# A conformer trunk step: the first two channel tiles projected from unscaled input

## The chip, the cores and the metric

The kernel runs as one program on one core of a Trainium2 chip. The metric is the device time of one execution in microseconds (us). The engines of the core work side by side, each through its own instructions in order: PE (TensorE, matmuls and weight loads), DVE (VectorE), ACT (ScalarE), POOL (GpSimd) and SP (SyncE), which here issues most DMAs.

## The reference, cut to what matters

Eight running streams of 16 new frames and one prompt of 512 frames go through a conformer layer, an attention layer and two feed-forward blocks. What the change touches is the head of the conformer layer:

```
def rms_norm(x, g):
    y = xf * lax.rsqrt(jnp.mean(xf * xf, axis=-1, keepdims=True) + EPS)
    return (y * g.astype(jnp.float32)).astype(x.dtype)

def conv_module(h, hist, g, w_pw1, b_pw1, w_dw, b_dw, ln_g, ln_b, w_pw2, b_pw2):
    a, gate = jnp.split(rms_norm(h, g) @ w_pw1 + b_pw1, 2, axis=-1)
    glu = a * jax.nn.sigmoid(gate)
    full = jnp.concatenate([hist.astype(glu.dtype), glu], axis=1)
    y = lax.conv_general_dilated(full, w_dw[:, None, :], ..., feature_group_count=D_MODEL) + b_dw
    y = jax.nn.silu(layer_norm(y, ln_g, ln_b))
    return h + y @ w_pw2 + b_pw2, full[:, -CONV_HIST:]
```

The model width is 1024. The factor of the norm, one number for each frame, is the same for all channels, so it may be multiplied in before or behind the projection; the gain `g`, one number for each input channel, must be in before it.

## The kernel before

**Layout.** Channels lie on the 128 partitions, in eight channel tiles (`KT`); frames lie along the free dimension. There are NT = 640 frames (128 of the streams, 512 of the prompt), cut into two groups of 320 (`GS`). `h` holds x. Every matmul that must be exact is made of three: an operand is split into a rounded high part and a low remainder (`xh`, `xl` of the input by `xsplit`, `whi`, `wlo` of the weights by `wsplit`), and `mm3` (lines 196 to 202) adds high by high, low weight by high input and high weight by low input. So one product of a tile of 128 output channels and a group takes 24 matmuls of 320 columns, and a channel tile of the gated projection, which has a value half and a gate half, takes 48 for each group.

**Order.** `PLAN` (line 72) is an order written out by hand, one letter for each step of `step` (line 987): `a0` is tile 0 for group 0, `y` loads the second half of x, `x1` is tile 1 for group 0 with the second group's norm inside it, `b0` and `b1` are tiles 0 and 1 for group 1, `q0` the depthwise convolution of tile 0 on POOL (`conv_pool`, whose inputs ACT makes), `dp1s0` a convolution on DVE, `c2` tile 2 for both groups, and so on. The tiling framework then places the instructions on the engines in the order of its own estimate; `high_priority` moves an instruction forward in it, and `behind` or `issue_after` ties an instruction behind another of the same engine, with no wait between engines.

**The first norm.** `rms` (line 292) calls `rstd_bc` (line 268): `square` for each tile of x on ACT or DVE (`SSQ`), a running sum `acc` on DVE for group 0 (`colmean`, line 219), three one-column matmuls that turn the sum into means, an added epsilon (`rst`, line 275), the power -1/2 on POOL (line 282), and `spread` (line 250), which copies the factor to all partitions in PSUM. Then, tile by tile, `n` (line 303) multiplies x, gain and factor on DVE, ACT rounds it to `xh` (line 187), and DVE makes `xl` (line 189). For group 1 the running sum is made on POOL. The first projection `glu_` (line 752) takes `xs[0]`, the result for group 0; the value half and the gate half are two `mm` tiles, of which there are four.

**Fillings.** `warm(n)` (line 143) issues n matmuls of the identity, each shown as two in the profile; `WARM = 30, 9, 5, 5` places them at the start, behind group 0's means, and behind each of the two spreads.

**Weights.** `wsplit` loads 1 MB for each tile into `raw` and splits it; for tiles 0 and 1 in four quarters (`cuts=4`, lines 732 and 737), whose order is tied to the norm's steps. `PL1 = (0, 2, ...)` puts half of tile 1's low parts on POOL. There are two buffers each of `raw`, `whi` and `wlo`.

**Tap weights.** `conv_load` (line 839) makes on POOL the tap weights of tiles whose convolution runs on PE, into three `w4` buffers. Those three buffers are used as scratch by the second group's norm before.

## Time and profile before

| what | value |
|---|---|
| median of 3 runs | 1464.73 us (1462.3 to 1465.26) |
| the profiled execution's own time | 1464.42 us |
| its span | 1462.5 us |
| PE busy | 1435.3 us, 98% of the span |
| DVE busy | 1141.8 us, 78% |
| ACT busy | 756.4 us, 52% |
| POOL busy | 294.4 us, 20% |
| data moved | 192.56 MB, 132 GB/s |

The span runs from the first to the last instruction that the profiler recorded; the rest of the time lies around it. In rows of stretches, each engine has its busy time and in brackets its number of instructions, then the granted clock of PE as a share, the DMA engines' share and the GB/s. In rows in order of time come the start, the length, the engine, the line of the kernel, the operation, what it writes and reads, the number of merged instructions, and in square brackets the idle time before it and what ended that.

### The profile page before, as it was taken

The numbers are of one execution on the slowest core, as the hardware profiler recorded it, in microseconds if no ns is written. First come the engines' busy times: TensorE is split into PE (matmuls) and PEld (weight loads), VectorE is DVE, ScalarE is ACT, GpSimd is POOL, SyncE is SP. The second block draws the span as 40 slices with busy tenths as digits, with TensorE's granted clock in tenths as the row PEclk, the third lists the DMA queues.
The fourth block names the chain that finished last, engine by engine and source line by source line (L and its number), as shares of the span: only waits on it lengthen the run. The fifth ranks groups of instructions, "written<-read, shape, count | busy, mean of one in ns | idle before, by whom it ended". The sixth has DMA issues, their size and how long they took to land.

```text
span 1462.5 us, 28255 instructions
## 1 busy us (share of the span) xinstructions
PE 1435.3 (98%) x11040; PEld 1371.7 (94%) x11040; DVE 1141.8 (78%) x2524; ACT 756.4 (52%) x1627; POOL 294.4 (20%) x349
## 2 busy tenths in 40 slices
PE   9999999999999999999999999999999999999998
PEld 8998799999999999999987898878999999999998
DVE  6789767899788789766768668576899888888755
ACT  4666544554554464445655455443565554455443
POOL 5699102011111111013222111011001111111101
PEclk9999999999999999999999999999999999999999
DMA  7267425045444445424655554461235444444522
GB/s 243 82 176 186 121 73 159 9 128 153 127 105 131 131 116 143 116 87 171 203 163 199 175 199 163 134 206 41 69 81 142 132 116 132 133 120 114 151 65 72
DMA packets 66932, 192.56 MB, mean 132 GB/s; under 512 B 12144, under 2 KB 30320, under 8 KB 58480
## 3 DMA queue, kind: packets, MB, share of 16 engines
q1 hardware_dynamic: 52432, 160.58, 33.9%
q0 software_dynamic: 13504, 29.37, 9.9%
q8 instruction: 86, 1.41, 0.4%
q10 hardware_dynamic: 864, 0.83, 0.2%
q14 instruction: 46, 0.38, 0.1%
HBM read 179.14 MB, written 11.61 MB: 130 GB/s over the span
## 4 chain that ended last, share of the span: by engine, by line
PE 75%; DVE 11%; POOL 4%; DMA 4%; issue 3%; ACT 3%; SPq 0%; DVEq 0%; POOLq 0%; ACTq 0%
PE mm L436 45%; PE mm L199 7%; PE mm L201 7%; PE mm L200 7%; POOL ca L830 3%; DVE w L820 2%; PE am L1307 1%; DMA raw<-in_w_in 1%; PE w L1323 1%; PE am L1354 1%; DVE wlo L370 1%; PE am L1290 1%; DVE hid L591 1%; PE w L1266 1%; PE mm L874 1%
## 5 line engine op out<-in xcount | busy, mean ns | idle before, releaser
L436 PE MATMUL mm<-XH,whi 128*128 128x320 f32 x896 | 275.8, 310 | 1.7 <-DVE t L451 0.7
L436 PE MATMUL mm<-XH,wlo 128*128 128x320 f32 x896 | 276.7, 309 | 0.0
L436 PE MATMUL mm<-XL,whi 128*128 128x320 f32 x896 | 274.7, 309 | 0.0
L369 ACT ACTIVATE whi<-raw 128x512 fp32r<-128x512 f32 (+2 forms) x280 | 169.2, 614 | 142.6 <-PE mm L436 114.3
L199 PE MATMUL mm<-xh,whi 128*128 128x320 f32 (+2 forms) x640 | 200.9, 315 | 1.2 <-ACT xh L187 0.8
L370 DVE TENSOR_TENSOR wlo<-raw,whi 128x512 fp32r<-128x512 f32 (+2 forms) x280 | 184.2, 666 | 21.4 <-ACT whi L369 20.2
L200 PE MATMUL mm<-xh,wlo 128*128 128x320 f32 (+2 forms) x640 | 198.9, 312 | 0.0
L201 PE MATMUL mm<-xl,whi 128*128 128x320 f32 (+2 forms) x640 | 197.1, 312 | 0.4 <-DVE xl L189 0.4
L436 PE MATMUL mm<-hid,whi 128*128 128x320 f32 x732 | 171.9, 310 | 2.4 <-DVE hid L370 2.2
L436 PEld LDWEIGHTS mm<-XH,whi 128*128 128x128 f32 x896 | 167.7, 188 | 3.4 <-ACT t L446 1.7
L436 PEld LDWEIGHTS mm<-XH,wlo 128*128 128x128 f32 x896 | 168.3, 188 | 0.0
L436 PEld LDWEIGHTS mm<-XL,whi 128*128 128x128 f32 x896 | 167.7, 188 | 0.0
L436 PEld LDWEIGHTS mm<-hid,whi 128*128 128x128 f32 x732 | 124.8, 188 | 4.7 <-DVE hid L370 3.2
L199 PEld LDWEIGHTS mm<-xh,whi 128*128 128x128 f32 x640 | 121.0, 189 | 4.4 <-ACT xh L187 2.0
L201 PEld LDWEIGHTS mm<-xl,whi 128*128 128x128 f32 x640 | 120.4, 189 | 1.3 <-DVE xl L189 0.8
L200 PEld LDWEIGHTS mm<-xh,wlo 128*128 128x128 f32 x640 | 121.1, 189 | 0.2
L436 PE MATMUL mm<-hid,wlo 128*128 128x320 f32 x366 | 113.0, 309 | 0.0
L436 PE MATMUL mm<-XL,shi 128*128 128x320 f32 x344 | 105.8, 309 | 2.1 <-DVE XL L370 2.1
L436 PE MATMUL mm<-XH,shi 128*128 128x320 f32 x344 | 106.1, 309 | 0.0
L436 PE MATMUL mm<-XH,slo 128*128 128x320 f32 x344 | 106.0, 308 | 0.0
L415 POOL DMA_DIRECT2D s<-in_w_in x38 | 22.0, 579 | 382.3 <-DVE wlo L370 205.5
L830 POOL TENSOR_TENSOR ca<-ca,cvt 128x512 f32<-128x512 f32 x60 | 91.9, 1532 | 17.7 <-ACT cvt L827 11.2
(272 smaller groups left out, 3367.0 us busy)
## 6 DMA issues: line engine op xcount, KB each, us to landing
raw<-in_w_in SPq DMA_DIRECT2D x38, 1024.0 KB
s<-in_w_in POOLq DMA_DIRECT2D x76, 256.0 KB, 4.2
raw<-in_w_os SPq DMA_DIRECT2D x24, 768.0 KB
cache<-in_ck SPq DMA_DIRECT2D x32, 512.0 KB
cache<-in_cv SPq DMA_DIRECT2D x32, 512.0 KB
raw<-in_w_pw SPq DMA_DIRECT2D x11, 1024.0 KB
s<-in_w_os POOLq DMA_DIRECT2D x48, 192.0 KB, 3.7
raw<-in_w_kq SPq DMA_DIRECT2D x8, 1024.0 KB
```

The lines of the kernel that those rows point to most:

```text
L199: nc.tensor.matmul(ps, wh, xh, start=(first and i == 0), stop=False)
L200: nc.tensor.matmul(ps, wl, xh, start=False, stop=False)
L201: end = nc.tensor.matmul(ps, wh, xl, start=False, stop=(stop and i == last))
L369: put_end[1] = nc.scalar.activation(out=hi, in_=src, func=AF.Copy).ins
L370: put_end[0] = nc.vector.tensor_tensor(out=lo, in0=src, in1=hi.bitcast(F32), op=sub).ins
L415: nc.gpsimd.dma_start(s1, src[:, 2 * n:3 * n])
L436: last = nc.tensor.matmul(pt, wt, v, start=(first and k == i == 0), stop=(k == n - 1 and i == 2), skip_group_check=True)
L591: nc.vector.scalar_tensor_tensor(out=t[k], in0=h[:, k0 + k, half * NH:half * NH + NH], scalar=col(V_NFFN + l * KT, k0 + k), in1=bcw[half], ...
L820: tap_end[0] = nc.vector.scalar_tensor_tensor(out=dst, in0=src, scalar=wj, in1=dst, op0=ALU.mult, op1=ALU.add).ins
L830: nc.gpsimd.tensor_tensor(out=acc, in0=acc, in1=pr, op=ALU.add)
L874: conv_end[0] = nc.tensor.matmul(pt[32 * q:32 * q + 32, 0:n], w4[0:r, 4 * tg + q, :], mv, start=(tg == 0), stop=(tg == 7)).ins
L1266: nc.tensor.matmul(ps, QQ[:, q], KK[:, 0:n], start=True, stop=False)
```

## The change

The first two channel tiles are projected, for group 0, from x times gain alone. `put_x` makes its high part on ACT (`ux[0]`, a scaled copy) and its low part on DVE (`ux[1]`). The squares of a pair of tiles go to PE at once, three one-column matmuls for each tile, with no running sum; `sum0` adds the 24 results, and the power follows. The factor is spread after the first half of tile 0's value product (`spread0`, which runs after all eight input tiles of the value half) and copied to SBUF by ACT (`bcx[0]`). In `glu_` two DVE products with that copy stand ahead of the activations for these two tiles. The second group's squares are summed on DVE instead of POOL; its means stand on PE behind the value half of tile 1 (`sums1`), its spread behind the first four input tiles of the gate half (`spread1`). Behind that spread come the second group's scaled input and then the first group's (`normal`), which the tiles from 2 on read; for the first group it takes the factor from the SBUF copy. Tile 0's second group takes value and gate in turns, input tile by input tile. The fillings become 7, 4, 3 and 2, all ahead of the first projection, between the squares. The second half of x is issued before the first history load. The `ux` tiles share the space of `y`, and the squares that of the tap weights, whose making is tied behind the first power.

```diff
--- before.py
+++ after.py
-PL1 = (0, 2, 0, 0, 0, 0, 0, 0)
+PL1 = (0, 0, 0, 0, 0, 0, 0, 0)
...
-WARM = 30, 9, 5, 5
+WARM = 7, 4, 3, 2
-PLAN = ("a0 y x1 b0 b1 q0 dp1s0 c2 ds1p2 D3 C4 S3 q3 C5 E6 u S4 A4 F6 u k ds2 B4 E7 e S5 A5 F7 f k k k S6 A6 "
+PLAN = ("y a0 x1 b0 b1 q0 dp1s0 c2 ds1p2 D3 C4 S3 q3 C5 E6 u S4 A4 F6 u k ds2 B4 E7 e S5 A5 F7 f k k k S6 A6 "
         "S7 A7 n s0 m w1")
...
-    def rms(g, gain, engs=SQ, cut=CUT, eng=nc.gpsimd, hold=None, hook=None):
+    def normal(g, gain, bc):
         n = gr[g][1]
-        bc, _ = rstd_bc([hp(g, k) for k in range(KT)], n, engs, cut, None, eng,
-                        accp=hold and hold(), hook=hook)
         xh, xl = new_xs(g)
-        if WARM[2 + g]:
-            with behind(norm_spread[0]):
-                warm(WARM[2 + g])
         for k in range(KT):
+            t = tp.tile([P, tw[0]], F32, tag="n1", name=nm("n1"), bufs=NB1)
             norm_end["n"].append(nc.vector.scalar_tensor_tensor(
                 out=t[:, :n], in0=hp(g, k), scalar=col(gain, k), in1=bc, op0=ALU.mult,
                 op1=ALU.mult).ins)
...
-    y = [cp.tile([P, KT, NH], F32, name=f"y{g}", tag=f"y{g}") for g in range(2)]
-
-    pws = {}
-
-    def first():
-        with behind(mean_end[0]):
-            warm(WARM[1])
-        pws[0] = wsplit(w_pw1[0], 16, P, cuts=4, pool=PL1[0],
-                        ties=[(norm_end["sq"], norm_end[e]) for e in ("acc", "acc", "rst", "rst")])
-
-    with tc.issue_after(warm(WARM[0])), tc.high_priority(offset=2 * HP):
-        xs = [rms(0, V_NCONV, SSQ, SCUT, nc.vector, hook=first), None]
-    pws[1] = wsplit(w_pw1[1], 16, P, cuts=4, pool=PL1[1],
-                    ties=(norm_end["sq"], norm_end["n"][3], norm_end["pow"]))
-    load_hist(0, 2)
-    nc.scalar.dma_start(dwv, vecs[:, V_N:])
+    ux = [cp.tile([P, KT, NH], F32R, name=f"ux{i}", tag=f"y{i}") for i in range(2)]
+    y = [None, None]
+    pws, xs, bcx = {}, [None, None], [None, None]
+
+    def tail_of(r, v=None):
+        norm_end["rst"] = nc.vector.tensor_scalar(out=r[:, :3], in0=r[:, :3] if v is None else v, scalar1=EPS,
+                                                  scalar2=None, op0=ALU.add).ins
+        r2 = tp.tile([P, 4], F32, tag="rst2", name=nm("rst2"))
+        norm_end["pow"] = nc.gpsimd.tensor_tensor(out=r2[:, :3], in0=r[:, :3], in1=mhalf[:, :3],
+                                                  op=ALU.pow).ins
+        return r2
 
     def w4t():
         return cp.tile([P, 1024], F32, tag="w4", name=nm("w4"), bufs=3)
 
+    def put_x(k, *tie):
+        with behind(*tie):
+            u = nc.scalar.activation(out=ux[0][:, k, :], in_=hp(0, k), func=AF.Copy,
+                                     scale=col(V_NCONV, k)).ins
+            return u, nc.vector.scalar_tensor_tensor(
+                out=ux[1][:, k, :], in0=hp(0, k), scalar=col(V_NCONV, k),
+                in1=ux[0][:, k, :].bitcast(F32), op0=ALU.mult, op1=ALU.subtract).ins
+
+    with tc.high_priority(offset=2 * HP):
+        st0, tl = w2t(), tiles(NH)
+        end, tie = warm(WARM[0]), ()
+        room = [w4t() for _ in range(3)]
+        for k in range(0, KT, 2):
+            with behind(*tie):
+                q = [square(hp(0, i), NH, SSQ[i], room[i // 3][:, i % 3 * NH:i % 3 * NH + NH])
+                     for i in (k, k + 1)]
+                if k + 2 == KT:
+                    tie = norm_end["sq"], tie[1]
+                else:
+                    put_x(k)
+                    tie = put_x(k + 1)
+            with tc.issue_after(end):
+                for i in (k, k + 1):
+                    for t, a in enumerate(tl):
+                        end = nc.tensor.matmul(st0[:, 512 + t * KT + i:513 + t * KT + i],
+                                               q[i - k][:, a:a + P], onec, start=True, stop=True).ins
+            if k + 2 < KT:
+                with tc.issue_after(end):
+                    end = warm(WARM[1 + k // 2])
+        first_end = end
+
+    def sum0():
+        r = tp.tile([P, 4], F32, tag="rst", name=nm("rst"))
+        nc.vector.tensor_reduce(out=r[:, :3], in_=st0[:, 512:512 + KT * 3].rearrange(
+            "p (t k) -> p t k", k=KT), op=ALU.add, axis=mybir.AxisListType.X)
+        return tail_of(r)
+
+    def split0(i):
+        if i == 1:
+            with tc.high_priority(offset=2 * HP):
+                u = put_x(KT - 2, norm_end["whi"], norm_end["wlo"])
+                return put_x(KT - 1, *u)
+        if i == 2:
+            with tc.high_priority(offset=2 * HP), behind(norm_end["wlo"]):
+                r0.append(sum0())
+            norm_end["pow0"] = norm_end["pow"]
+        return tie if i == 0 else (norm_end["whi"], norm_end["rst"])
+
+    r0 = []
+    pws[0] = wsplit(w_pw1[0], 16, P, cuts=4, ties=split0)
+    pws[1] = wsplit(w_pw1[1], 16, P, cuts=4, ties=(norm_end["whi"], norm_end["wlo"]))
+
+    def spread0(last):
+        with tc.issue_after(last):
+            end = spread(st0, r0[0], NH, True)
+        bcx[0] = cp.tile([P, T], F32, tag="cvt", name=nm("cvt"), bufs=CVT)[:, :NH]
+        with tc.high_priority(offset=2 * HP):
+            norm_end["bc"] = nc.scalar.activation(out=bcx[0], in_=st0[:, :NH], func=AF.Copy).ins
+        return end
+
+    half1 = []
+
+    def sums1(last):
+        st = w2t()
+        with behind(last, norm_end["bc"]):
+            r, v = colmean(st, [lambda k=k: square(hp(1, k), NH, "a") for k in range(KT)], NH, KT,
+                           "rst", nc.vector)
+        half1[:] = st, tail_of(r, v)
+        return mean_end[0]
+
+    def spread1(last):
+        st, r2 = half1
+        with tc.issue_after(last):
+            end = spread(st, r2, NH, True)
+        xs[1] = normal(1, V_NCONV, st[:, :NH])
+        xs[0] = normal(0, V_NCONV, bcx[0])
+        return end
+
+    nc.scalar.dma_start(dwv, vecs[:, V_N:])
+
     glu_end, gate_end, conv_end, sum_end, store_end, read_end, tap_end = ([None] for _ in range(7))
 
     def glu(c, g, wh, wl, mid=None):
-        glu_(c, g, wh, wl, mid)
+        glu_(c, g, wh, wl, mid or {}, None if mid is None else ux)
         if g == 0:
             nc.sync.dma_start(convs_out[:, c], gs[:, c])
 
-    def glu_(c, g, wh, wl, mid):
+    def glu_(c, g, wh, wl, mid, raw=None):
         n = gr[g][1]
-        ps = []
-        for ab in range(2):
-            pt = mmt()
-            mm3(pt[:, :n], [(wh[:, (ab * 8 + k) * P:(ab * 8 + k + 1) * P],
-                             wl[:, (ab * 8 + k) * P:(ab * 8 + k + 1) * P]) for k in range(KT)],
-                xk(xs[g], range(KT)))
-            ps.append(pt[:, :n])
-            if mid and ab == 0:
-                mid()
+        ps, last = [mmt()[:, :n], mmt()[:, :n]], first_end if c == 0 and raw else None
+        seq = [(ab, range(o, o + 4)) for ab in range(2) for o in (0, 4)]
+        if c == 0 and g:
+            seq = [(ab, range(k, k + 1)) for k in range(KT) for ab in range(2)]
+        for ab, ks in seq:
+            with tc.issue_after(last) if last else nullcontext():
+                end = mm3(ps[ab], [(wh[:, (ab * 8 + k) * P:(ab * 8 + k + 1) * P],
+                                    wl[:, (ab * 8 + k) * P:(ab * 8 + k + 1) * P]) for k in ks],
+                          xk(raw or xs[g], ks), ks[0] == 0, ks[-1] == KT - 1)
+            if raw:
+                last = mid.get((ab, ks[0]), lambda e: e)(end.ins)
         with tc.high_priority(offset=HP):
             t = tp.tile([P, tw[0]], F32, tag="t1", name=nm("t1"))
+            a = tp.tile([P, tw[0]], F32, tag="t2", name=nm("t2"))
+            if raw:
+                for i, out in enumerate((a, t)):
+                    nc.vector.tensor_tensor(out=out[:, :n], in0=ps[i], in1=bcx[0], op=ALU.mult)
+                ps = a[:, :n], t[:, :n]
             glu_end[0] = nc.scalar.activation(out=t[:, :n], in_=ps[1], func=AF.Tanh, scale=0.5,
                                               bias=hb1[:, KT + c:KT + c + 1]).ins
-            a = tp.tile([P, tw[0]], F32, tag="t2", name=nm("t2"))
             nc.scalar.activation(out=a[:, :n], in_=ps[0], func=AF.Identity, scale=0.5,
                                  bias=hb1[:, c:c + 1])
             ns = 0 if g else NB * SB
...
-        nc.gpsimd.tensor_tensor(
-            out=w4, in0=i4[:, None, :].to_broadcast([P, 32, 32]),
-            in1=dwv[:, V_DW4 + 32 * c:V_DW4 + 32 * c + 32].unsqueeze(2).to_broadcast([P, 32, 32]),
-            op=ALU.mult)
+        with behind(norm_end["pow0"]):
+            nc.gpsimd.tensor_tensor(
+                out=w4, in0=i4[:, None, :].to_broadcast([P, 32, 32]),
+                in1=dwv[:, V_DW4 + 32 * c:V_DW4 + 32 * c + 32].unsqueeze(2).to_broadcast(
+                    [P, 32, 32]), op=ALU.mult)
         return w4
...
-            glu(c, 0, *pws[c])
+            glu(c, 0, *pws[c], mid={(0, 4): spread0})
         elif op == "b":
             glu(c, 1, *pws[c])
         elif op == "c":
...
         elif op == "y":
             load_x(1)
+            load_hist(0, 2)
         elif op == "x":
-            def mid():
-                with behind(norm_end["xh"][2], norm_end["pow"]):
-                    xs[1] = rms(1, V_NCONV, SSQ1, 8, hold=w4t)
-            glu(1, 0, *pws[1], mid=mid)
+            glu(1, 0, *pws[1], mid={(0, 4): sums1, (1, 0): spread1})
+            for g in range(2):
+                y[g] = cp.tile([P, KT, NH], F32, name=f"y{g}", tag=f"y{g}")
         elif op in "CDEF":
             if op != "F":
                 load_hist(c, c + 1)
                 w4 = conv_load(c) if c + 1 < KT else None
                 if c + 1 < KT:
                     pws[c + 1] = wsplit(w_pw1[c + 1], 16, P, late=op == "E")
-                glu_(c, 0, *pws[c], None)
+                glu_(c, 0, *pws[c], {})
                 if op == "E" and c + 1 < KT:
                     with behind(gate_end[0], glu_end[0]):
                         pws[c + 1] = pws[c + 1]()
```

31 lines of the change are left out of this document (14 added, 17 removed).

## The prediction

> **What bounds the kernel now.** I read the page first, then busy time by stretch, then the start of every engine in order of time, since the edit touches the first two channel tiles only.
>
> ```profile
> span 1462.5 us, 28255 instructions
> PE 1435.3 (98%) x11040; PEld 1371.7 (94%) x11040; DVE 1141.8 (78%) x2524; ACT 756.4 (52%) x1627; POOL 294.4 (20%) x349
> ...
> 0.00:15.19 15.19, 13.12 (x101) 12.89 (x101) 8.42 (x19) 8.65 (x16) 5.42 (x18) 1.00 0.88 304
> 15.19:42.54 27.35, 25.43 (x170) 24.19 (x171) 21.66 (x39) 11.37 (x28) 15.21 (x12) 1.00 0.56 162
> 42.54:51.24 8.70, 8.70 (x62) 8.70 (x61) 4.03 (x4) 8.70 (x13) 4.28 (x4) 1.00 0.38 121
> ...
> 80.00:150.00 70.00, 70.00 (x759) 64.81 (x761) 65.87 (x124) 42.79 (x69) 63.95 (x42) 1.00 0.66 174
> ```
>
> PE works 98% of the span, and after 42.54 us it is busy without a break up to 150. So time is gained only where PE does nothing useful, or is late. Both lie at the start:
>
> ```profile
> 1.63 8.54 PE L146 MATMUL mm<-ident 128*128 128x128 f32 x60 [1.63 <-POOL ident masks.py:199]
> ...
> 15.19 0.41 PE L199 MATMUL mm<-xh,whi 128*128 128x320 f32 x1 [0.44 <-ACT xh L187]
> ...
> 21.45 0.41 PE L199 MATMUL mm<-xh,whi 128*128 128x320 f32 x1 [0.35 <-ACT xh L187]
> ...
> 27.03 0.78 PE L238 MATMUL w<-onec,w 128*128 128x1 f32 x6
> 29.01 0.93 PE L252 MATMUL w<-ident,rst 128*128 128x128 f32 x6 [1.20 <-POOL rst L282]
> 29.78 1.28 PE L146 MATMUL mm<-ident 128*128 128x128 f32 x10
> 30.81 0.39 PE L199 MATMUL mm<-xh,whi 128*128 128x320 f32 x1
> ...
> 37.00 0.56 PE L201 MATMUL mm<-xl,whi 128*128 128x320 f32 x2 [0.37 <-DVE xl L189]
> ```
>
> Everything on PE before 15.19 is filling (L146) or the norm; the first projection starts there. Behind it are three idles (0.35, 1.20, 0.37) and ten filling matmuls (1.28).
>
> **The earlier start.** The projection no longer waits for the norm's factor but for gain-scaled halves of x and the first quarter of the weights:
>
> ```profile
> 2.26 5.74 DMA h<-in_xa
> 8.02 6.10 DMA raw<-in_w_pw
> ...
> 4.15 0.47 ACT L208 ACTIVATE sq<-h 128x320 f32<-128x320 f32 x1 [1.19 <-DMA h<-in_xa]
> ...
> 8.27 1.00 ACT L208 ACTIVATE sq<-h 128x320 f32<-128x320 f32 x2 [0.98 <-DVE acc L229]
> 9.18 2.17 ACT L175 ACTIVATE whi<-raw 128x512 fp32r<-128x512 f32 x4
> ...
> 9.88 1.29 DVE L180 TENSOR_TENSOR wlo<-raw,whi 128x512 fp32r<-128x512 f32 x2
> ...
> 18.55 0.88 DVE L189 TENSOR_TENSOR xl<-n,xh 128x320 fp32r<-128x320 f32 x2
> ...
> 185.27 0.17 DVE L242 TENSOR_REDUCE mst<-w 128x3 f32<-128x12 f32 x1 [1.23 <-PE w L238]
> ...
> 11.31 1.25 POOL L282 TENSOR_TENSOR rst<-rst,mhalf 128x3 f32<-128x3 f32 x1 [8.74 <-DVE rst L275]
> ...
> 60.00:80.00 20.00, 20.00 (x138) 20.00 (x138) 17.40 (x33) 12.92 (x19) 19.05 (x13) 1.00 0.36 112
> ```
>
> x lands in four pieces between 4.15 and some 8.2. ACT now has per piece one or two squares and two scaled copies, about 0.45 us each, which fit between the pieces; the last copies stand behind the first weight quarter. So ACT squares the last piece at 8.27 to 9.2 as before and makes the first high quarter 9.2 to 9.75 (2.17/4 = 0.54). DVE makes its low part until 10.5 (0.65 each). PE can run from 10.5, against 15.19: **4.7 us** earlier. The 24 one-column matmuls of the squares are in groups of six (0.78) in gaps where PE waits for x, and end near 10.0: nothing on the path. Without that cover they would cost 4 x 0.78 = 3.1.
>
> Next: x's last two low parts and the second low quarter take DVE to 12.05 (0.44 twice, 0.65); PE's second twelve matmuls start at 10.5 + 12 x 0.145 = 12.2 (20.00/138 each), so they run through to 14.0. The sums' reduction (0.17), its epsilon and the power (1.25) start at 12.05 and end near 13.7, before 14.0. The factor's spread then costs PE its own time, **-0.9** (0.93, as at 29.01). In place of DVE's products with the factor, which stood ahead of the start, come two products for each of the two tiles behind their projections; PE does not wait for those, it has two more result buffers.
>
> **What else goes from PE's path.** The ten filling matmuls: **+1.3**. The three idles, as far as nothing takes their place: 0.35 + 1.20 + 0.37 = **+1.9**. Gross gain: 4.7 - 0.9 + 1.3 + 1.9 = **7.0 us**. Four things can take it back.
>
> **A, the sums of the second group.** They stand in PE's order behind the first half of tile 1: 14.0 + 0.9 + 24 + 24 matmuls (7.0) = 21.9. Their seven adds move from POOL to DVE; PE waits in order, with half a tile's work behind. x's second half is now issued ahead of the first history load:
>
> ```profile
> 8.71 0.38 SPq L711 DMA_DIRECT2D gall<-in_hist  x1
> 9.38 3.09 SPq L118 DMA_DIRECT2D h<-in_xb  x4
> ```
>
> It lands no later than before, and the history is not needed until tile 0's gate, near 20, so the swap costs nothing; each microsecond by which that load came after 20 would hold DVE at the gate. If DVE is free it ends the adds by 19. But POOL's three tap-weight products now follow the first power at once:
>
> ```profile
> 32.38 2.10 POOL L841 TENSOR_TENSOR w<-i,dwv 128x1024 f32<-128x1024 f32 x1 [1.55 <-DVE xl L189]
> ...
> 32.62 2.21 DVE L189 TENSOR_TENSOR xl<-n,xh 128x320 fp32r<-128x320 f32 x1
> 34.75 2.20 DVE L189 TENSOR_TENSOR xl<-n,xh 128x320 fp32r<-128x320 f32 x1
> ```
>
> The two subtractions take 2.2 us beside POOL's products, 0.44 without them: one DVE operation passes per POOL operation. From 13.7 to 20.0 DVE would get three low quarters of tile 1 through; the fourth and seven adds end at 20.0 + 0.65 + 7 x 0.44 = 23.7, with tile 0's products and gates (about 1.7) before them 25.4. A lies between 0 and 3.5; I take 1.3, under the middle, since the adds alone give 1.8 and POOL holds DVE only where it comes first.
>
> **B, feeding the second group.** Tile 0's second group asks for one channel tile of x per six matmuls (0.87), while DVE needs a product and a low part for each:
>
> ```profile
> 13.67 1.01 DVE L303 SCALAR_TENSOR_TENSOR n<-h,vec,w 128x320 f32<-128x320 f32 x2 [1.24 <-PE w L252]
> ...
> 27.93 0.29 DVE L774 SCALAR_TENSOR_TENSOR gall<-t,t 128x128 f32<-128x128 f32 x1
> 28.14 0.35 DVE L781 SCALAR_TENSOR_TENSOR gall<-t,t 128x192 f32<-128x192 f32 x1
> ```
>
> 0.5 + 0.44 = 0.94, with a lead of 12 matmuls (1.7), and tile 1's two products and its gates (2 x 0.5 + 0.29 + 0.35, some 1.7 as for tile 0) in between: 0 to 1.5; taken 0.3, since ACT needs a microsecond between products and gates in which DVE goes on.
>
> **C, the clock.** The fillings shrink from 30, 9, 5, 5 to 7, 4, 3, 2:
>
> ```profile
> 183.08 2.15 PE L238 MATMUL w<-onec,y 128*128 128x1 f32 x18
> ...
> 186.18 0.47 PE L199 MATMUL mm<-xh,whi 128*128 128x320 f32 x1
> 186.45 0.47 PE L200 MATMUL mm<-xh,wlo 128*128 128x320 f32 x1
> ...
> 180.00:200.00 20.00, 20.00 (x136) 20.00 (x135) 12.39 (x25) 10.15 (x18) 0.00 (x0) 0.91 0.15 53
> ```
>
> Behind a stretch of one-column matmuls PE ran at half rate: starts 0.27 apart instead of 0.145, with 0.91 granted over those 20 us, so half speed for about 20 x 0.09 x 2 = 3.6 us. Such a stretch loses half of its length, 1.8. Against it, the 0.78 + 1.20 from 27.03 to 29.01 left the next matmuls at full rate. In the new start about 2 us of 8 are fillings after the first block. 0 to 1.8; taken 0.4. The Trainium skill ("TensorE: Matmul & The Clock Gate", part 1, "What's actually happening") says that the gate opens after a busy window of about 3.4 us and closes after an idle one; the 3.6 us here agree, and by it the price would be half a window, an estimate of 1.7.
>
> **D, the scaled input of the other six tiles.** It moves from the start to behind the second group's: sixteen DVE operations (eight products, eight low parts) and eight ACT copies, now due when tile 2 begins.
>
> ```profile
> 45.23 0.81 ACT L827 ACTIVATE ca<-gall,vec,dwv 128x512 f32<-128x512 f32 x1
> ...
> 44.42 2.36 DVE L180 TENSOR_TENSOR wlo<-raw,whi 128x1024 fp32r<-128x1024 f32 x2 [0.45 <-ACT whi L175]
> ...
> 51.24 1.13 DVE L817 TENSOR_SCALAR w<-gall,dwv,vec 128x512 f32<-128x512 f32 x2
> ...
> 46.72 29.25 POOL L830 TENSOR_TENSOR ca<-ca,cvt 128x512 f32<-128x512 f32 x18 [10.12 <-ACT cvt L827]
> ```
>
> Count from S, the second spread's end. PE: half of tile 1's second product (1.7), tile 0's and tile 1's second groups (7.0 each): tile 2 begins at S + 15.7 and needs the last of its eight x tiles 21 matmuls later, at S + 18.8. DVE: 7.5 for the second group, 1.7 for tile 1, 0.5 for a gate, 2.4 for tile 2's low weights (now before its input), 7.5 for this input: S + 19.6. So even undisturbed it is 0.8 late. Then POOL's taps: they began at 46.72, 4.2 behind the second group's end at 42.54, thus near S + 13, while twelve of the sixteen operations are still to come. Each of these has both operands in SBUF (the products too, as the factor is now a copy and no longer PSUM). One that waits out a tap (29.25/18 = 1.6 as they come, less its own 0.47) loses up to 1.1. But ACT makes the taps' inputs in the same order as x's high parts, so a held DVE holds the next taps back as well, and where DVE comes first POOL is the one to wait. Bounds 0.0 (if PE itself arrives late by A to C) and 12 x 1.1 = 13; taken **1.5**, the 0.8 and about one such wait, nearer the low end because DVE idles 8.70 - 4.03 = 4.7 us from 42.54 to 51.24 and can use that.
>
> On those pairs the Trainium skill ("SBUF — State Buffer", "Who interferes with whom") states that a DVE instruction with two SBUF inputs contends with a GpSimd one that reads SBUF, and the later one blocks entirely. The 2.21 against 0.44 agrees; taken literally for all twelve it gives the last rival below.
>
> PL1 adds half of tile 1's low weights to DVE (2 x 0.65 = 1.3); they are made between 13 and 16, due at 18.4, and cost nothing unless POOL holds DVE, which A contains.
>
> **The sum.** 7.0 - 1.3 - 0.3 - 0.4 - 1.5 = 3.5 us. The profiled execution took 1464.42 (its span 1462.5 and 1.92 around it), so 1460.9; the median shown is 0.31 above it: **1461.2**. From tile 2 on the operations are the same, DVE, POOL and PE all start earlier by about the same, so I let the shift stay to the end.
>
> **Rivals.**
> 1. *Nothing takes it back.* A to D at zero: 1464.7 - 7.0 = 1457.7. For it: DVE idles 5.7 of the 27.35 us from 15.19 to 42.54. Against: the 2.2 us subtractions.
> 2. *The gain goes into the second group's sums and the clock.* A at 3.5, C at 1.8, B 0.3, D 0.8: 0.6 left, 1464.1. For it: PE has nothing else in its order there. Against: only two of twelve adds and low parts are seen held so long.
> 3. *Slower: POOL's taps against the moved input.* With A to C as taken, 5.0 are left for D, so it decides from the moment D passes 5.0, when four of the twelve operations wait a whole tap (0.8 + 4 x 1.1). With seven, D is 8.5 and the time 1464.7 + 3.5 = 1468.2. For it: the taps run without a break after 46.72, and DVE's chains are what the later stage waits for (65.87 of 70 us). Against: ACT's order throttles the taps.
> 4. *The change does not bring the start forward*, since PE waits until both low quarters and x's last low parts are there (12.05) and starts near 13: gross 4.5, net 1.0, 1463.7; counted with rival 2.
>
> **Chances.** Forecast 0.55, its own range 1458.8 to 1463.2; rival 1 0.17; rivals 2 and 4 0.15; rival 3 0.13. A measurement tells 0.2% from nothing, 2.9 us: faster means under 1461.8, slower over 1467.6. Of the forecast 0.43 lies below 1461.8, 0.12 above. Faster 0.43 + 0.17 = 0.60, same 0.12 + 0.15 = 0.27, slower 0.13. The range runs from 1456.5 (rival 1, and the half-rate stretch near 186, which may fall otherwise when all shifts) to 1466.0, which leaves out the outer part of rival 3.
>
> **What would show it.** The first L199-type matmul near 10.5 and the first spread near 14 show the start right. A is PE's wait ahead of the second group's one-column matmuls, near 22. D is PE's idle in tile 2's first twenty matmuls, with low parts of x over 1 us beside L830's successor. C is starts 0.27 apart between 10 and 18. The last matmul of tile 1's second group, the start of POOL's taps and DVE's first tap, now 46.72 and 51.24, should each move by 3 to 7 us. If they do and the end does not, the later stage has swallowed it; if PE's first start stays above 13, the working fails at its first step.

## The result and the profile after

The changed kernel takes 1468.48 us in the median (1466.76 to 1469.56, 7 runs), the kernel before 1463.03 us over the runs made beside it (1462.13 to 1465.26, 7 runs). The ratio is 1.0035, with a 95% interval of 1.0023 to 1.0046: slower by 3 to 7 us, where 3.5 us less were forecast. The profiled execution of the changed kernel took 1466.76 us, the fastest of its seven, while that of before (1464.42) was among its slower ones; so the two profiles differ by 2.3 us where the medians differ by 5.4.

The head of the page of the changed kernel, then its busy time by stretch (columns as before):

```profile
span 1464.9 us, 28213 instructions
PE 1437.3 (98%) x11016; PEld 1374.8 (94%) x11016; DVE 1148.7 (78%) x2537; ACT 760.6 (52%) x1636; POOL 286.5 (20%) x338
...
10.00:20.00 10.00, 10.00 (x47) 10.00 (x48) 5.98 (x10) 4.14 (x9) 3.75 (x3) 0.56 1.05 368
...
30.00:40.00 10.00, 9.66 (x58) 9.66 (x59) 5.74 (x15) 2.88 (x6) 0.85 (x1) 0.83 0.37 139
```

PE is as busy as it was, but from 10 to 20 us it got 47 instructions through where the kernel before had 72, at a granted clock of 0.56. PE in order of time shows with what:

```profile
1.64 3.35 PE L146 MATMUL mm<-ident 128*128 128x128 f32 x14 [1.64 <-POOL gall L716]
4.78 1.57 PE L760 MATMUL w<-onec,w 128*128 128x1 f32 x12
...
9.77 2.56 PE L760 MATMUL w<-onec,w 128*128 128x1 f32 x12
...
13.19 2.56 PE L760 MATMUL w<-onec,w 128*128 128x1 f32 x12
15.61 0.61 PE L201 MATMUL mm<-ux,whi 128*128 128x320 f32 x1
16.02 0.47 PE L202 MATMUL mm<-ux,wlo 128*128 128x320 f32 x1
16.29 0.47 PE L203 MATMUL mm<-ux,whi 128*128 128x320 f32 x1
...
30.34 0.83 PE L240 MATMUL w<-onec,acc 128*128 128x1 f32 x6 [1.82 <-DVE acc L231]
...
33.21 1.49 PE L254 MATMUL w<-ident,rst 128*128 128x128 f32 x6
34.35 0.61 PE L201 MATMUL mm<-ux,whi 128*128 128x320 f32 x1
34.77 0.47 PE L202 MATMUL mm<-ux,wlo 128*128 128x320 f32 x1
...
67.60 0.42 PE L201 MATMUL mm<-xh,whi 128*128 128x320 f32 x1 [2.06 <-ACT t L845]
```

The reader is to see four things. The squares' matmuls are four blocks of twelve records, since each such matmul leaves two, and the later blocks take 2.56 us, 0.21 for each record. The first projection starts at 15.61, later than the 15.19 of before, and runs with starts 0.27 apart. Ahead of the second group's sums PE waits 1.82 for DVE, and the half rate returns behind it. At 67.60 PE waits once more, for ACT, which had stood behind POOL's taps.

DVE and POOL in the same profile:

```profile
16.08 8.86 DVE L181 TENSOR_TENSOR wlo<-raw,whi 128x512 fp32r<-128x512 f32 x6
...
17.47 6.91 POOL L916 TENSOR_TENSOR w<-i,dwv 128x1024 f32<-128x1024 f32 x3
...
54.83 1.60 DVE L191 TENSOR_TENSOR xl<-n,xh 128x320 fp32r<-128x320 f32 x1 [1.27 <-ACT xh L189]
```

The six low parts of weights, 0.65 us each when alone, take 8.86 beside POOL's three products.

The convolution stage is best followed by the first and last start of three groups: POOL's taps, DVE's taps, and the first kind of PE's convolution matmuls. A row of one source line has the shortest, median and longest duration in ns, then first and last start. The kernel before:

```profile
L830 POOL TENSOR_TENSOR ca<-ca,cvt x60: 1276/1301/3342, 46.7 to 148.9; 128x512 f32<-128x512 f32 x60
...
L820 DVE SCALAR_TENSOR_TENSOR w<-gall,dwv,w x150: 337/356/756, 55.7 to 154.9; 128x128 f32<-128x128 f32 x90, 128x512 f32<-128x512 f32 x60
...
L874 PE MATMUL mm<-xa,w x576: 270/273/329, 91.5 to 159.3; 128*32 128x128 f32 x93, 128*32 128x192 f32 x75, 96*32 96x128 f32 x14, 96*32 96x192 f32 x10
```

And the changed kernel:

```profile
L904 POOL TENSOR_TENSOR ca<-ca,cvt x60: 1264/1300/3869, 53.3 to 154.0; 128x512 f32<-128x512 f32 x60
...
L894 DVE SCALAR_TENSOR_TENSOR w<-gall,dwv,w x150: 339/356/756, 62.3 to 158.6; 128x128 f32<-128x128 f32 x90, 128x512 f32<-128x512 f32 x60
...
L949 PE MATMUL mm<-xa,w x576: 270/273/328, 96.0 to 162.9; 128*32 128x128 f32 x93, 128*32 128x192 f32 x75, 96*32 96x128 f32 x14, 96*32 96x192 f32 x10
```

POOL's and DVE's taps begin 6.6 us later and end 5.1 and 3.7 later; PE's convolution ends 3.6 later. So the taps' delay is there before the stage begins, and the stage hands on a little over half of it. Here and below, DVE's first tap is the first of the row shown (55.7 before), not the single product that opens the chain, which the prediction took (51.24 before, 58.34 now).

Tile 0's second group, which releases POOL's taps, ended near 42.5 before and near 47.7 now. The order in which PE's instructions stand in the two programs, from that group's first matmul to its last, shows one reason that no row of durations shows:

```
before: 48 of tile 0's second group,  3 of tile 1's among them
after:  48 of tile 0's second group, 29 of tile 1's among them
```

Presumably the planner's estimate has DVE feed tile 0 more slowly than it does, and fills the gaps that it foresees with tile 1. In the profile of e5_b0first, where the 29 are moved away, PE has no such gap, so in the changed kernel tile 0 ends up to 26 x 0.147 = 3.8 us later for them. Whether the kernel's time suffers by it is another question, and e5 answers it.

### The profile page after: what moved, and what is told of

It reads as the page before. It is cut to its first block, busy times and chain, and to the rows that moved or that the text cites. A ratio compares the mean times of both kernels' runs of the same rounds, so it can differ in the third digit from the quotient of the medians.

```text
span 1464.9 us, 28213 instructions
## 1 busy us (share of the span) xinstructions
PE 1437.3 (98%) x11016; PEld 1374.8 (94%) x11016; DVE 1148.7 (78%) x2537; ACT 760.6 (52%) x1636; POOL 286.5 (20%) x338
## 4 chain that ended last, share of the span: by engine, by line
PE 84%; DVE 7%; ACT 4%; DMA 3%; POOL 1%; issue 1%; SPq 0%; DVEq 0%; POOLq 0%; ACTq 0%
PE mm L432 48%; PE mm L201 9%; PE mm L203 8%; PE mm L202 8%; PE mm L949 2%; PE am L1382 1%; PE w L1398 1%; PE am L1365 1%; ACT whi L164 1%; PE am L1429 1%; DVE hid L587 1%; DVE wlo L366 1%; PE w L240 1%; DMA raw<-in_w_in 1%; PE w L1341 1%
## 5 line engine op out<-in xcount | busy, mean ns | idle before, releaser
L201 PE MATMUL mm<-xh,whi 128*128 128x320 f32 (+2 forms) x608 | 190.6, 315 | 2.7 <-ACT t L845 2.1
L202 PE MATMUL mm<-xh,wlo 128*128 128x320 f32 (+2 forms) x608 | 189.1, 312 | 0.0
L203 PE MATMUL mm<-xl,whi 128*128 128x320 f32 (+2 forms) x608 | 186.4, 312 | 0.0
L201 PEld LDWEIGHTS mm<-xh,whi 128*128 128x128 f32 x608 | 115.0, 189 | 5.8 <-ACT t L845 2.3
L202 PEld LDWEIGHTS mm<-xh,wlo 128*128 128x128 f32 x608 | 115.1, 190 | 0.3
L203 PEld LDWEIGHTS mm<-xl,whi 128*128 128x128 f32 x608 | 114.4, 189 | 0.3 <-issue 0.2
```

Of the source, the lines that this page charges most:

```text
L201: nc.tensor.matmul(ps, wh, xh, start=(first and i == 0), stop=False)
L202: nc.tensor.matmul(ps, wl, xh, start=False, stop=False)
L203: end = nc.tensor.matmul(ps, wh, xl, start=False, stop=(stop and i == last))
```

## The experiments

The edits are against the changed kernel unless said otherwise. Times are medians; each ratio is to the kernel before, in the runs made beside it.

| run | edit | us | ratio and interval |
|---|---|---|---|
| e1_few | few fillings | 1467.88 | 1.0032 (1.0021 to 1.0043) |
| e2_wide | sums 128 columns wide | 1465.68 | 1.0022 (1.0012 to 1.0031) |
| e3_late | tap weights later | 1468.57 | 1.0037 (1.0025 to 1.0050) |
| e4_acc | sums on DVE | 1470.91 | 1.0053 (1.0038 to 1.0068) |
| e5_b0first | tile 1 behind tile 0 | 1468.12 | 1.0035 (1.0021 to 1.0049) |
| e7_wide_b0 | e2 and e5 | 1466.72 | 1.0025 (1.0013 to 1.0036) |
| e6_all | e2, e3 and e5 | 1465.36 | 1.0018 (1.0008 to 1.0029) |
| e8_all_few | e6 and few fillings | 1463.81 | 1.0003 (0.9993 to 1.0012) |
| e9_raw | all tiles unscaled | 1470.85 | 1.0056 (1.0040 to 1.0072) |
| e10_raw_all | e8 and e9 | 1463.29 | 1.0004 (0.9994 to 1.0013) |
| e11_raw_early | e10 without e3 | 1465.09 | 1.0017 (1.0007 to 1.0026) |
| e12_taps_behind | e8, taps behind the copy | 1464.19 | 1.0002 (0.9994 to 1.0011) |
| e13_before_cold | the kernel before, first filling 7 | 1467.14 | 1.0027 (1.0015 to 1.0039) |

**e1_few: are the fillings in the way?**

```diff
-WARM = 7, 4, 3, 2
+WARM = 1, 1, 1, 1
```

> The changed kernel with the fillings cut from 7, 4, 3, 2 to 1, 1, 1, 1 (32 records become 8). Theory 1 (the one-column matmuls of the squares are 48 records on PE, they run at half rate, about 0.21 us each, and they alone fill PE up to the first projection): the start stays near 15 (4.9 + 48 x 0.21 = 15.0) and the time stays within 2 us of the changed kernel, 1468. Theory 2 (the fillings between them are what delays the start): 24 records of about 0.2 fewer, the start falls to some 11 and the time by about 4.

1467.88, as the changed kernel. PE in order of time:

```profile
13.85 2.56 PE L760 MATMUL w<-onec,w 128*128 128x1 f32 x12
16.27 0.61 PE L201 MATMUL mm<-ux,whi 128*128 128x320 f32 x1
```

All four blocks now ran at half rate (2.56 to 2.72 us each), so the start did not come forward. In the changed kernel the first two blocks had still run at full rate (1.57 and 1.40); what the missing fillings saved went to the lost rate. The run shows that fewer fillings alone do not help; it does not show that they cost nothing, and e8 below, at full rate, gains by a similar cut.

**e2_wide: is it the one column that costs the rate?** The same number of records, 128 columns wide.

```diff
+        onew = room[2][:, 640:640 + P]
+        nc.gpsimd.memset(onew, 1.0 / D)
...
-                        end = nc.tensor.matmul(st0[:, 512 + t * KT + i:513 + t * KT + i],
-                                               q[i - k][:, a:a + P], onec, start=True, stop=True).ins
+                        end = nc.tensor.matmul(st0[:, 512 + i * 3 + t:512 + i * 3 + t + P],
+                                               q[i - k][:, a:a + P], onew, start=True, stop=True).ins
...
-            "p (t k) -> p t k", k=KT), op=ALU.add, axis=mybir.AxisListType.X)
+            "p (k t) -> p t k", k=KT), op=ALU.add, axis=mybir.AxisListType.X)
```

> The changed kernel with the matmuls of group 0's squares made 128 columns wide (ones in all of them, the same sums in each column, one kept): same number of records, but PE's array is busy. Theory 1 (half rate because one-column matmuls leave the array idle): the rate stays full from about 5 us on, 0.10 us a record, the first projection starts near 12 instead of 15.6 and runs with starts 0.147 apart from its first matmul on; 4 to 5 us less, about 1463.5. Theory 3 (what is lost lies behind the start, in the waits for DVE beside POOL): the start moves but the wait ahead of the second group's sums grows by as much, and the time stays within 1.5 us of 1468.

PE in order of time:

```profile
4.96 2.45 PE L762 MATMUL w<-w,w 128*128 128x128 f32 x12
...
11.94 1.50 PE L762 MATMUL w<-w 128*128 128x128 f32 x12
13.20 0.39 PE L201 MATMUL mm<-ux,whi 128*128 128x320 f32 x1
13.43 0.31 PE L202 MATMUL mm<-ux,wlo 128*128 128x320 f32 x1
13.58 0.31 PE L203 MATMUL mm<-ux,whi 128*128 128x320 f32 x1
...
28.05 1.44 PE L240 MATMUL w<-onec,acc 128*128 128x1 f32 x6 [3.37 <-DVE acc L231]
```

A block of twelve falls from 2.56 to 1.50 although 128 columns stream instead of one, the start from 15.61 to 13.20, and the projections stand 0.15 apart at once. The time falls by 2.8 (1.9 by the ratios), less than the 4 to 5 that theory 1 wanted, and the wait ahead of the second sums grows from 1.82 to 3.37, as theory 3 said. Both are at work.

That it is the columns, and not chance in a single execution, shows in all the profiles. In the seven with wide sums (e2, e6, e7, e8, e10, e11, e12) every block after the first takes 1.50 to 1.60 and the first projection stands between 10.90 and 13.20, at full rate. In the five with one column (the changed kernel, e1, e3, e5, e9) the last two blocks take 2.56 and the first projection stands between 15.61 and 18.82, at half rate.

**e3_late: POOL's products away from DVE's low parts.**

```diff
         half1[:] = st, tail_of(r, v)
+        norm_end["pow0"] = norm_end["pow"]
```

> The changed kernel with the tap-weight products on POOL tied behind the second power instead of the first. Theory 3 (DVE held by POOL from 17.5 to 24.4 makes PE wait at the second group's sums): six low parts of the weights take 4 us instead of 8.9, the 1.8 us wait and the half-rate stretch behind it (about 1.5) vanish, 2 to 3 us less, about 1465.5. Theory 1: the start stays at 15.6; only that wait may go, and some of it comes back beside the second group's low parts (2.2 instead of 0.44): 0 to 2 us less.

The wait ahead of the sums went, yet the time stayed, 1468.57. In the profiled execution, whose first spread stood at 22.24 instead of 20.65, PE came to its 97th projection matmul 2.1 us ahead of the changed kernel (34.82 against 36.87), but to the 145th only 0.8 ahead (43.07 against 43.91): POOL's products now ran beside the second group's low parts, as theory 1 had said. Together with an earlier start the edit counts: e6_all against e7_wide_b0, below, and e10 against e11.

**e4_acc: the running sum back on DVE.**

```diff
-WARM = 7, 4, 3, 2
+WARM = 30, 4, 3, 2
...
-                        end = nc.tensor.matmul(st0[:, 512 + t * KT + i:513 + t * KT + i],
-                                               q[i - k][:, a:a + P], onec, start=True, stop=True).ins
+            qs += q
...
+        for i in range(1, KT):
+            nc.vector.tensor_tensor(out=qs[0], in0=qs[0], in1=qs[i], op=ALU.add)
...
-            glu(c, 0, *pws[c], mid={(0, 4): spread0})
+            glu(c, 0, *pws[c], mid={(0, 4): means0, (1, 0): spread0})
```

> The changed kernel with group 0's squares summed on DVE again (seven adds behind the first two weight quarters), three matmuls for the sums behind the value half of tile 0, the spread behind the first half of its gate product, and a first filling of 30 as before the change. Theory 1: first projection near 10.5 at full rate, some 5 us ahead of the changed kernel and 1.5 more for the rate; DVE's 3.1 us of adds may cost 1 to 2 at the third weight quarter; 3 to 5 us less than the changed kernel, 1463.5 to 1465.5. Theory 3: no more than 1.5 less.

PE in order of time:

```profile
10.96 0.39 PE L201 MATMUL mm<-ux,whi 128*128 128x320 f32 x1
11.20 0.31 PE L202 MATMUL mm<-ux,wlo 128*128 128x320 f32 x1
...
18.61 1.44 PE L768 MATMUL w<-onec,w 128*128 128x1 f32 x6 [3.88 <-DVE w L762]
```

The start came as theory 1 had it, at 10.96 and at full rate; the time did not: 1470.91, a miss for both. PE waited 3.88 us for DVE ahead of the sums, then went on at half rate, and the spread came at 25.16. With the seven adds in its order DVE was not done before 18.6. An early first projection alone did not shorten the time.

**e5_b0first: tile 0 ahead of tile 1.**

```diff
-    half1 = []
+    half1, b0_end = [], [None]
...
+        if c == 1 and g:
+            last = b0_end[0]
...
+            if c == 0 and g:
+                b0_end[0] = end.ins
```

> The changed kernel with the matmuls of tile 1's second group tied behind the last of tile 0's second group; 29 of them stood ahead of it. Theory 4 (POOL's tap chain of tile 0 sets the pace of the convolution stage, it takes some 101 us wherever it starts, and tile 0's second group, which releases it, ends 4.3 us late because of those 29): tile 0's second group ends near 44 instead of 47.7, POOL's first tap moves from 53.3 to about 49, the first convolution on PE ends 3 us earlier, and the time falls by 3 to 4 us to some 1464.5. Rival (PE is the bound, so the order of its work changes nothing): within 1 us of 1468, and PE idles while DVE feeds tile 0.

1468.12, no change, though the order was mended. The profiled execution shows two things. First, its start, whose code is that of the changed kernel, came later by clock alone:

```profile
9.11 2.56 PE L760 MATMUL w<-onec,w 128*128 128x1 f32 x12
...
18.79 0.61 PE L201 MATMUL mm<-ux,whi 128*128 128x320 f32 x1
19.20 0.47 PE L202 MATMUL mm<-ux,wlo 128*128 128x320 f32 x1
19.46 0.47 PE L203 MATMUL mm<-ux,whi 128*128 128x320 f32 x1
...
36.04 0.83 PE L254 MATMUL w<-ident,rst 128*128 128x128 f32 x6
```

Second, counted from the second spread, POOL's taps now start 51.4 - 36.0 = 15.4 us behind it, against 53.3 - 33.2 = 20.1, so the tie does what it should. But now more of them run beside the second scaled copy; the chain goes from 51.4 to 156.4, 105.0 long instead of 100.7, and DVE's first tap came at 65.2, 29.2 behind the spread as in the changed kernel (62.3 - 33.2 = 29.1). What POOL wins, DVE does not. Theory 4 in its simple form fell, and no cost of the 29 matmuls to the kernel's time is shown.

**e7_wide_b0, e6_all, e8_all_few: the edits together.** e6_all has e2's, e3's and e5's edits, e7_wide_b0 leaves out e3's, and e8_all_few has fewer fillings beside:

```diff
-WARM = 7, 4, 3, 2
+WARM = 7, 1, 1, 1
```

> The same tie, with the 128-column sums of e2_wide. Theory 4: the two gains add, POOL's first tap near 48, 5 to 6 us less than the changed kernel, 1462.5 to 1463.5, about level with the kernel before. Rival: no better than e2_wide, 1465.7.

> The same tie and the 128-column sums, and the tap-weight products behind the second power as in e3_late. Theory 4 with the POOL lock: the wait ahead of the second group's sums (3.4 us in e2_wide) goes, its spread ends near 28.5 instead of 34, tile 0's second group near 39 to 41 (some low parts of x beside POOL at 2.2 us), POOL's first tap at 43.5 to 46; 1460 to 1462.5, faster than the kernel before. Rival: the products on POOL cost as much at the low parts of x as they cost at the sums, same as e7_wide_b0.

> e6_all with the fillings between the sums cut from 4, 3, 2 to 1, 1, 1 (12 records of about 0.10 us fewer on PE ahead of the first projection). Theory 1: first projection 1 us earlier than e6_all at full rate, and if nothing else waits 0 to 1 us less; if the array is then too idle, half rate returns and it is 1 to 2 us more.

1466.72, 1465.36 and 1463.81. e7 is no better than e2 alone, as the rival said. e6 missed the 1460 to 1462.5 expected of it. e3's edit, worth nothing by itself, gives 1.4 here: the six low parts take 3.70 us in e6 and 8.86 in e7, by DVE in order of time. First e6_all, then e7_wide_b0:

```profile
13.12 3.70 DVE L181 TENSOR_TENSOR wlo<-raw,whi 128x512 fp32r<-128x512 f32 x6
```

```profile
13.39 8.86 DVE L181 TENSOR_TENSOR wlo<-raw,whi 128x512 fp32r<-128x512 f32 x6
```

e8's fewer fillings give 1.5 more: with wide sums the rate stays full without them, and the first projection starts at 11.51 (12.55 in e6):

```profile
11.51 0.40 PE L201 MATMUL mm<-ux,whi 128*128 128x320 f32 x1
```

So the four edits together take back 4.7 of the 5.4 us. The columns, POOL's products beside DVE's low parts and the fillings each show a part of it; the order of tile 0 and tile 1 shows none, since neither e5 nor e7 gained by it and no run leaves it alone out of e8. But e8 is level with the kernel before, not faster as e6 was expected to be, although its first projection is 3.7 us ahead. DVE in e8:

```profile
44.31 3.10 DVE L299 SCALAR_TENSOR_TENSOR n<-h,vec,cvt 128x320 f32<-128x320 f32 x2
47.34 3.09 DVE L191 TENSOR_TENSOR xl<-n,xh 128x320 fp32r<-128x320 f32 x2
```

1.5 us for an operation of 0.5, beside POOL's taps: this is the term D of the prediction. DVE's first tap comes at 58.1, behind the 55.7 of before.

**e9_raw, e10_raw_all, e11_raw_early: no second scaled copy.** All eight tiles of group 0 are projected from the unscaled input.

```diff
-    ux = [cp.tile([P, KT, NH], F32R, name=f"ux{i}", tag=f"y{i}") for i in range(2)]
+    ux = new_xs(0)
...
-        xs[0] = normal(0, V_NCONV, bcx[0])
...
-            if raw:
+            if g == 0:
                 for i, out in enumerate((a, t)):
```

> The changed kernel with all eight tiles of group 0 projected from the unscaled input: the second scaled copy of it (eight products, eight low parts on DVE, eight copies on ACT) goes, tiles 2 to 7 get two DVE products with the factor each (12 x 0.48 = 5.8 us, spread over the stage, one operand in PSUM). Theory 5 (the stage is set by DVE: its tap chain takes 96 us from its first tap, and the second scaled copy, held by POOL's taps, stands ahead of that): DVE's first tap moves from 62.3 to some 54 to 56, the first convolution on PE ends 3 to 6 us earlier, the time falls by 3 to 6 us to 1462 to 1465. Rival (the late start of PE, 15.6 us and half rate, sets it): PE's first part is the same, so no more than 1 us of gain.

> The same on top of e8_all_few (128-column sums, few fillings, tap weights behind the second power, tile 1's second group behind tile 0's). Theory 5: DVE's first tap from 58.1 to 50 to 53; with chains of 96 us the first convolution ends near 153 to 155 against 159.3 before the change, and the time is 1457 to 1461, faster than both kernels. Rival: at most 1 us below e8_all_few, 1463.

> e10_raw_all with the tap-weight products behind the first power again. Theory 3: the wait of 3.4 to 3.8 us ahead of the second group's sums returns, tile 0's second group is fed without waits, so 1 to 2 us more than e10_raw_all. Rival: POOL's 6.9 us cost DVE as much in either place, no difference beyond 0.7 us.

1470.85, 1463.29 and 1465.09. e9 is a miss: its first spread stood at 24.40 in the profiled execution, the longest of its four. Counted from the second spread (36.09) DVE's first tap does come earlier, 61.9 - 36.1 = 25.8 against 29.1, and still PE's convolution ends at 168.1 instead of 162.9. In e10 DVE's first tap does come at 51.1, 7 us ahead of e8, and still the time is that of e8 and of before: its taps end at 153.2, 102 us after the first. Theory 5's fixed length of 96 us is wrong. e10's waits between 40 and 155 us (who waits for whom, total, times, longest):

```profile
POOL ca L910 <- ACT cvt L907: 20.8, 4, 13.0
...
ACT t L851 <- DVE t L847: 5.6, 2, 3.1
...
ACT t L849 <- DVE t L847: 2.4, 2, 1.9
```

The new products stand between PE and ACT; ACT, in order, waits for them 8.0 us, and POOL waits for ACT 20.8 - 13.0 = 7.8 us beyond its first wait. e11 pays 1.8 more than e10 for POOL's products beside the low parts, with a 3.94 us wait ahead of the sums: e3's edit confirmed once more.

**e12_taps_behind: the taps behind the copy.**

```diff
-            copy, rest = conv_pool(c)
+            with behind(split_end[0]) if c == 0 else nullcontext():
+                copy, rest = conv_pool(c)
```

> e8_all_few with ACT's inputs for POOL's first tap chain tied behind the last high part of the second scaled copy, so that POOL's taps do not run beside it. Theory 6 (the two hold each other up: 1.5 us for a DVE operation beside a tap against 0.5 without): the products and low parts take 0.5 us each, the copy ends near 49 instead of 61, DVE's first tap comes near 50 instead of 58.1, POOL's first tap near 49 instead of 44.3; with POOL's chain back at 101 us its end stays near 150 and DVE's taps end by 150; 1 to 4 us less than e8_all_few, 1460 to 1463. Rival (POOL's chain alone sets the stage, from its first tap): the 4.7 us by which it starts later are lost, 1466 to 1468.

DVE in e12, the same operations as in e8:

```profile
43.75 1.01 DVE L299 SCALAR_TENSOR_TENSOR n<-h,vec,cvt 128x320 f32<-128x320 f32 x2
44.83 0.95 DVE L191 TENSOR_TENSOR xl<-n,xh 128x320 fp32r<-128x320 f32 x2
```

They are back at 0.5, so POOL's taps were what held them. DVE's first tap comes at 51.8, but POOL's only at 54.9, because the tied copy's last part itself waited for DVE until 53; POOL's chain is then 99.3 long. Both end near 154 again, and the time, 1464.19, is that of e8. The theory holds for the single operations and fails for the total.

Where the lead goes can be counted from the traces: when PE starts its 1st, 97th, 145th, 241st, 289th and 337th projection matmul, and its last convolution matmul. Where nothing holds PE, 48 of them take 7.04 us.

| profile | 1st | 97th | 145th | 241st | 289th | 337th | convolution's last |
|---|---|---|---|---|---|---|---|
| before | 15.19 | 34.42 | 42.09 | 56.17 | 63.21 | 70.25 | 159.3 |
| changed | 15.61 | 36.87 | 43.91 | 58.34 | 67.60 | 74.74 | 162.9 |
| e8_all_few | 11.51 | 27.69 | 39.25 | 53.37 | 63.55 | 70.71 | 159.3 |
| e12_taps_behind | 11.88 | 28.06 | 38.69 | 52.77 | 59.81 | 66.85 | 158.3 |
| e10_raw_all | 11.10 | 27.27 | 38.81 | 52.89 | 59.93 | 66.97 | 158.5 |

e8 leads the kernel before by 6.7 us at the 97th. It loses 3.9 of it by the 145th, where the second group's input is made beside POOL's products (11.56 us for 48), and 3.1 more between the 241st and the 289th (10.18), beside the second scaled copy. e12 and e10 take that second loss away (7.04), and so carry a lead of 3.3 to 3.4 into the convolution; its end keeps 0.8 to 1.0 of it.

**e13_before_cold: the half rate by itself, in the kernel before.**

```diff
-WARM = 30, 9, 5, 5
+WARM = 7, 9, 5, 5
```

> The kernel before the change with its first filling cut from 30 to 7, nothing else. Theory 1 (without enough work in the array before the first projection PE runs it at half rate): PE idles from 4 to 10 us, the sums, spread and the first 12 to 25 projections run at half rate, 1.5 to 3 us more than before, 1465 to 1466. Rival (the start waits for data, the rate is of no account): the time stays within 0.7 us of before, 1463.2.

PE in order of time:

```profile
10.00 1.44 PE L238 MATMUL w<-onec,acc 128*128 128x1 f32 x6 [5.01 <-DVE acc L229]
11.31 3.58 PE L146 MATMUL mm<-ident 128*128 128x128 f32 x18
...
31.02 2.20 PE L146 MATMUL mm<-ident 128*128 128x128 f32 x10
32.87 0.61 PE L199 MATMUL mm<-xh,whi 128*128 128x320 f32 x1
33.29 0.47 PE L200 MATMUL mm<-xh,wlo 128*128 128x320 f32 x1
```

1467.14, ratio 1.0027 (1.0015 to 1.0039): 3.8 us for nothing but 23 fillings left out while PE had no other work. The nine fillings behind the sums take 3.58 instead of 2.25, the first projection moves from 15.19 to 16.7, and a second half-rate stretch falls on the projections at 33. The first filling bought its rate.

## Why the prediction was wrong

**The earlier start: the step that failed.** The prediction said of the squares' matmuls that they "are in groups of six (0.78) in gaps where PE waits for x, and end near 10.0: nothing on the path". The row it was taken from, x6 in 0.78, was three matmuls with two records each, so a pair of tiles is twelve records, not six; and it was a row at full rate. Forty-eight records at up to 0.21, with the fillings between them, keep PE busy without a break until 15.6, and they are the path. The gain of 4.7 became a loss of 0.4. What was worked out for DVE's part of the start was right: the first low part of tile 0's weights was ready at 10.27 in the changed kernel (forecast 10.5) and the second at 11.80 (forecast 12.05), and the first projection stood at 10.96 in e4, with the sums moved behind it, and at 11.51 in e8, with wide ones.

**C, the clock: right in kind, too small, and not added to the start.** It was taken at 0.4 with a bound of 1.8. In the profile of the changed kernel twelve projections from 15.61 and some seven more and the spread at 33.2 ran at half rate, 19 x 0.12 and 0.6 or about 2.9 us, and the half rate of the sums comes on top. e13 prices less filling at the start, with its consequences, at 3.8. The Trainium skill ("TensorE: Matmul & The Clock Gate", part 1, "What's actually happening") has the clock follow how busy PE has been; e13 agrees, and the runs add that one-column matmuls do not hold the full rate, though PE is busy with them by its record: e2 changes their width, and the rate holds.

**A, the second group's sums: right in kind, taken too low.** PE's arrival was forecast near 21.9, with 0 to 3.5 us of wait, taken 1.3. In the changed kernel PE came at 28.5, 6.6 us late, and still waited 1.82; where it comes earlier, it waits 3.37 (e2), 3.75 (e7) and 3.94 (e11, sums at 26.31, near the 25.4 of the upper bound). e3 and e6 show that POOL's products are what makes it.

**B, feeding the second group: hidden in the changed kernel, too low in the repaired one.** In the changed kernel PE has no wait there, but it had 29 matmuls of tile 1 to do in between. The order was not foreseen; nothing of the trace before shows an order that is still to be planned. That it cost time is not shown: e5 takes the 29 away and gains nothing. Where PE comes early, in e8, the 97th to the 145th matmul take 11.56 instead of 7.04, for waits of 2.2 us in all for x and a half rate behind them: 4.5 more, at a place that was priced at 0.3. The products on POOL, charged to A alone, fall there once they are moved away from the sums.

**D, the moved input: right in kind.** Taken at 1.5 in bounds of 0 to 13. Operations that take 0.5 take 1.5 beside the taps (e8 against e12), in agreement with the rule of the Trainium skill that was quoted for it ("SBUF — State Buffer", "Who interferes with whom"); the rival that the prediction takes from that rule is its third, not its last. On PE it costs 2.2 us in the changed kernel (9.26 for the 48 from the 241st on, against 7.04) and 3.1 in e8. In the kernel's time it does not show: taking it away in e12 or e10 moves DVE's first tap by 6 to 7 us and the time by less than 1.

**The sum and the rivals.** The sign was wrong because 4.7 us of gain at the start never came and the half rate came on top: PE is 2.2 us behind the kernel before at its 241st projection matmul, and 4.4 at its 289th, behind D. But the start is not the whole error. In e8 it comes 3.7 us early, and the time is only level with the kernel before; the forecast 3.5 us of gain are lost there at B and D, and where D is taken away in the convolution, which in e10 and e12 keeps a third of PE's lead or less, where the prediction let the whole shift stay to the end. The third rival gave 1468.2, close to the 1468.48 measured, but by luck: its 8.5 us were to be paid at D, which took 2.2 on PE. The fourth, that the start does not come forward, was the right one, for another reason than given, and was priced too gently at 13 us and 1463.7. The sentence on what would prove the working wrong, a first start above 13, is what the profile shows; the starts of the taps, which were to come 3 to 7 us earlier, came 6.6 and 7.1 later.

**What stays open.** Why the taps end near 154 in e8, e10 and e12, although their first ones stand up to 7 us apart, was not settled; POOL's wait for ACT is a reason that holds for e10 only. The 1.2 us between the convolution's delay (3.6) and that of the profiled span (2.4) were not followed up; what follows the start of the last convolution matmul took between 1299.9 and 1305.3 us in the profiles, and the first spread of the same code stood between 20.65 and 24.59, which is more than that.

## What to carry to other kernels

Count matmuls by records of the same type of operand before pricing more of them, and price small ones at the rate that PE has where they stand, not at that of the row they come from. Work that looks like idle filling may be what holds the rate: try the filling alone before taking it away. An earlier start is worth only what the next shared stage lets through: follow PE's place in its order, matmul by matmul, to see where a lead goes. When work is moved to an engine's idle time, look at who runs beside it there, and at the order that the planner then makes of everything it can see.

## What the runs showed of the hardware that was not expected

- One-column matmuls run PE down to half rate, although it is busy by its own record: twelve take 1.40 to 1.57 us while the rate is still full and 2.56 later on, against 1.50 for twelve that stream 128 columns (e2).
- The half rate falls at other places from one execution to the next: the same code ran two of its four blocks at full rate and started its first projection at 15.61 in one, and ran none of them so and started at 18.79 in another (e5).
- The granted clock of a stretch is not always to be trusted for this. In e5's row below, from 10 to 20 us, it is 1.00, while twelve records take 2.56 us there:

```profile
10.00:20.00 10.00, 10.00 (x47) 10.00 (x47) 2.87 (x8) 4.55 (x9) 0.57 (x1) 1.00 1.06 374
```
